# One store for both DRAM copies of a query or key half, with a channel's four copies side by side

## The chip, the cores and the metric

The kernel runs on one core of one Trainium2 chip. The metric is the device time of one execution in microseconds (us), as a median over runs. The core has five instruction queues: PE (TensorE, matmuls), DVE (VectorE), ACT (ScalarE), POOL (GpSimd) and SP (SyncE, which here issues nearly all DMAs). Each works through its instructions in the order of the program and waits on semaphores. SBUF is the on-chip memory of 128 partitions, PSUM the matmuls' accumulators, DRAM (HBM) the memory off the core.

## The reference, cut to what matters

Two layers of a hybrid block run over 1024 latent tokens and 256 context tokens. One of each layer's mixers is a differential attention of 4 heads with 2 softmaxes each, so 8 pairs of query and key with 32 channels:

```
q, k, v = split_qkv(pb, L)                 # from the shared input projection
q = apply_rope(q, rope_cos, rope_sin)      # latent tokens only
k = apply_rope(k, rope_cos, rope_sin)
keys = jnp.concatenate([k, k_c], 1)        # context keys behind the latent ones
s = jnp.einsum('bqhcd,bkhcd->bhcqk', q, k).astype(jnp.float32) * (DIFF_DK ** -0.5)
p = jax.nn.softmax(s, -1)
w = p[:, :, 0] - lam * p[:, :, 1]
return jnp.einsum('bhqk,bkhd->bqhd', w, v)
```

The other mixers are a recurrence (RG-LRU), a convolution module and a long convolution (hyena). A mixture of experts follows. All inputs are float32.

## The kernel before, in words

**Precision by halves.** A float32 number is carried as two fp32r numbers, a high half (hi) and the rest (lo). A pair's 32 channels of q are laid out as 128 rows hi, hi, lo, lo, those of k as hi, lo, hi, lo, so that one matmul over 128 rows adds all four products. That layout is made through DRAM: the tensor `qkd` has, for q (kind 0) and k (kind 1) and each of the 8 pairs, four copies of 32 channels by 1280 tokens, of 5,120 bytes a row.

**Phase 1 of a layer** (`phase1`) does the input projection, block by block of 128 columns (`win`). The matmuls (L1065) need the block's weights: a 512 KB load (`wir`, one buffer), split by ACT (`wih`, L948) and POOL (`wil`, L951), with two buffers of each half. The tokens come in groups of 512, 512 and 256 (the last is the context; in layer 1 q leaves it out). A group's result is evacuated from PSUM by a function of the block's kind. For q and k that is `qk_evac`, on 128 channels (4 pairs) at a time, so i = 0 and i = 1 for q and for k: ACT copies PSUM to `qf` (L1075), DVE shuffles and POOL and DVE apply the rotation (L1078 to L1081), ACT makes `qhi` (L948), POOL makes `qlo` (L951), and SP stores them to `qkd` (L1087), each half twice. `qhi`, `qlo` and `qf` have two buffers each, so a group's halves can be made only when the stores of the group before the last have landed.

Beside i = 0 the recurrence of the second channel block runs on DVE, POOL and ACT (`rglru`, tiles `rg_...`, L1401 to L1424), with the convolution's multiply-adds on DVE (`cacc`, L1448). Behind k of i = 1 PE goes on with the recurrence's gate (`rglru_out`, tiles `stg`, L1435 to L1437) and hyena's first block (`d_evac`, L1126), whose weights are one more `wir` load.

**Attention** (`attention`) begins with SP's loads of the constants (`lamv`, `subg`), of four `ks` (128 rows by 1280 tokens, L1269) and seven `qs` (128 by 256, L1276), all from `qkd`; a pair's 128 rows are one piece of DRAM. Then come the scores (`A`, L1186).

**What sets the order.** Every engine's program is fixed by a scheduler before the run. On SP the stores, the `wir` loads and the attention's loads stand in one order, so a load waits until all stores ahead of it have been issued.

Of the kernel before, what the change touches and what calls it, by code (L numbers as in the profile page):

```python
# [13 lines left out]
def rope_tables():  # L14
    rows = SEQ // GRID_W
    row = np.repeat(np.arange(rows, dtype=np.float32), GRID_W)
    col = np.tile(np.arange(GRID_W, dtype=np.float32), rows)
    inv = (np.float32(10000.0) ** (-np.arange(ROPE_FREQS, dtype=np.float32) / np.float32(ROPE_FREQS))).astype(np.float32)
    ang = np.concatenate([row[:, None] * inv, col[:, None] * inv], -1).astype(np.float32)   # [L, 16]
    c, s = np.cos(ang).T, np.sin(ang).T  # L20
    cos = np.tile(np.concatenate([c, c], 0), (4, 1))
    sin = np.tile(np.concatenate([-s, s], 0), (4, 1))
    return np.stack([cos, sin]).astype(np.float32)      # [2, 128, L]


def feats(L):
# [5 lines left out]
    return np.ascontiguousarray(f.T), tu                # [33, L], [L]  # L32


# Long convolution over n = 2048 points, split by k = 8 q + r, t = 256 a + p.
# Slots of 128 frequencies: 0: r0 (q < 128), 1: r4, 2-3: r1, 4-5: r2, 6-7: r3.
SLOT_R = [(0, 0), (4, 0), (1, 0), (1, 1), (2, 0), (2, 1), (3, 0), (3, 1)]
# what the butterflies give: real part and imaginary part with a sign
# [3 lines left out]
class Bank:  # L42
# [11 lines left out]
    def array(self):  # L54
        return np.ascontiguousarray(np.stack(self.blocks, 1))    # [128, nb, 128]


def long_tables():
# [3 lines left out]
    plan_f = []          # per slot: (re list, im list) of (input, half, block)  # L62
    for s, (r, qb) in enumerate(SLOT_R):
        q = np.arange(128) + 128 * qb
        th = 2 * np.pi * np.outer(p, 8 * q + r) / n       # [p, q]
        C, S = np.cos(th), np.sin(th)
        re, im = [], []
        for h in range(2):
            sl = slice(h * 128, h * 128 + 128)
            if r == 0:  # L70
                re.append(("a0", h, fw.add(C[sl])))
                m = -S[sl].copy()
                m[:, 0] = np.cos(np.pi * p[sl])           # k = 1024 in the place of Im of k = 0
# [11 lines left out]
    plan_i = {}          # per output: per half: list of (part, slot, block)  # L85
# [27 lines left out]
def short_tables():  # L113
    """n = 512, 256 times: slots 0: k < 128 (and k = 256 in Im's first row), 1: 128 <= k < 256."""
# [31 lines left out]
def pieces(tabs, long):  # L146
    """The tables' blocks in the order of their use, 8 to a piece, and where each product finds its block."""
# [24 lines left out]
def conv_tables():  # L172
    """The long convolution's tables, each frequency group's complex products as three real ones, in pieces of 4
    blocks in the order of use: forward, then inverse. Per group its pieces, each with two lists of
    (input, half, block) or (input, slot, block)."""
# [17 lines left out]
    # real inputs: both slots' real parts, then their imaginary parts  # L193
    lists = []
    for im in range(2):
        for r in (0, 4):
            C, S = trig(r, 0)
            m = -S if im else C
            if im and r == 0:
                m[:, 0] = np.cos(np.pi * p)          # k = 1024 in the place of Im of k = 0  # L200
            lists.append([(f"a{r}", h, m[half(h)]) for h in range(2)])
    fw.append(pieces_of(lists))
    # re = C (r + g i) + g (S - C) i, im = C (r + g i) - (C + S) r
# [6 lines left out]
    # inverse  # L210
# [10 lines left out]
    # R = C (Yr + Yi) - (C + S) Yi, I = C (Yr + Yi) + (S - C) Yr  # L221
# [7 lines left out]
    # the short ones  # L229
# [18 lines left out]
P = 128  # L248
# [5 lines left out]
def bcast_rows(ap1d, n, parts=P):  # L254
    """A DRAM vector of n elements as [parts, n], each partition the same."""
# [3 lines left out]
def moe_consts(K, nfix):  # L259
# [5 lines left out]
    K.j16 = c.tile([P, 8], FT, name="j16")          # j + 16  # L265
    iota(K.j16, [[1, 8]], 16)
    # falling order of the experts of the same count, those of fixed steps ahead: along the row, down the partitions
# [5 lines left out]
    # column (f, i): i in the partitions of f, -1 in the others  # L273
# [11 lines left out]
    iota(d, [[1, P]], 0, -1)                        # col - part  # L285
    K.tri = c.tile([P, P], BF, name="tri")          # tri[t', t] = t' < t
# [3 lines left out]
    K.half = c.tile([P, 1], FT, name="half")        # 1 in partitions 64 and up  # L290
# [8 lines left out]
class Router:  # L299
    """The lists of each step's tokens, from the logits of one block of tokens after the other.  # L300

    The first nfix steps take the experts of that number, the others the rest by falling count; step i has
    caps[i] rows, in blocks of 128 and, for up to 64, a last one of 64."""

    def __init__(self, K, l, NB, caps, nfix, keep, w, lists):
# [6 lines left out]
        self.OH = keep.tile([P, NB, 2, NE], BF, name="rOH")     # either choice's expert  # L312
        self.ra = keep.tile([P, NB, 2], FT, name="rra")         # its rank among the expert's
        # row + 1, token + 1, gate, the gate's low part
# [4 lines left out]
        self.cnt = keep.tile([P, 4, NE], BF, name="rcnt")       # of the rows so far, by partition  # L319
# [5 lines left out]
    def first_max(self, x, n, oh, neg):  # L325
        """One-hot oh of the first of x's largest, whose negative goes to neg"""
# [9 lines left out]
    def choose(self, b, lg):  # L336
        """The two experts of a block's tokens and their gates"""
# [9 lines left out]
        # logits of the chosen group  # L347
# [25 lines left out]
    def place(self, b):  # L373
        """A block's assignments into the lists [(value, expert), rank]"""
# [3 lines left out]
        # ranks: the rows above in the block and those of the blocks before  # L378
# [24 lines left out]
    def finish(self):  # L403
# [9 lines left out]
        # each expert's position, and the permutation  # L413
# [11 lines left out]
        # the lists as they are, and the first 64 rows of each block twice  # L425
# [11 lines left out]
        # 2**20 in rows of no assignment; half rows in blocks of 64, the first half in the lower partitions  # L437
# [6 lines left out]
        # the order of the experts last: the first rows are wanted ahead of more weights  # L444
# [11 lines left out]
    def beyond(self):  # L456
        """Whether any expert has more rows than its step"""
# [1855 lines left out]
```

## Time and profile before

| | us |
|---|---|
| median of 3 runs | 3641.28 |
| lowest and highest run | 3637.17, 3642.21 |
| span of the profiled execution, first to last instruction | 3627.2 |

Of the profiled execution the page gives the span alone; it is 14.1 us under the median of the runs, which is the work around the span together with the spread of runs. Over the span PE is busy 84%, DVE 63%, ACT 43% and POOL 20%, the DMA engines 55.8% by the hardware queue. These are means over stages with different limits. The change touches phase 1 of either layer, which in the trace lies at about 425 to 611 us and 2200 to 2367 us. A row of the trace begins with its start, then its duration; what stands in brackets behind it is the idle time of the engine before it and what ended that time. PEclk is the granted clock of TensorE as a share of its full 2.4 GHz. The DMA share is the mean busy share of the core's 16 DMA engines.

### The profile page before, as it was taken

What the parts mean: (1) busy time and instruction counts of PE and PEld (TensorE: products, weight loads), DVE (VectorE), ACT (ScalarE), POOL (GpSimd) and SP (SyncE); (2) the same over time, 40 slices, a digit from 0 to 9 for tenths busy, and PEclk for the clock granted to TensorE, in tenths of its full rate; (3) what the DMA queues carried; (4) which work ended last, traced back from release to release, by engine and by line L of the source; (5) the groups of instructions that cost most, each with busy time, mean ns of one, the idle gap of its engine ahead of it and who ended that gap; (6) DMA issues with size and microseconds to landing.
All of it is one profiled execution on the core that took longest, in us unless ns stands there. A gap on an engine that the chain in (4) does not pass through costs nothing. (4 is left out here: it accounts for less than half of the span.)

```text
span 3627.2 us, 43878 instructions
## 1 busy us (share of the span) xinstructions
PE 3060.8 (84%) x14952; PEld 2066.6 (57%) x14952; DVE 2269.4 (63%) x3297; ACT 1564.9 (43%) x2537; POOL 717.3 (20%) x579
## 2 busy tenths in 40 slices
PE   5898775998789699999998587789888799899993
PEld 1246664676568354577554465557667665465552
DVE  6675873887768444375543678478886753356626
ACT  4234342774324233365543454267433344345523
POOL 2213441001320101111110444300230111111102
PEclk9999987999999699999999798889989899999996
DMA  6751224223566789996978512221446389978796
GB/s 189 225 196 49 69 85 159 81 73 128 168 197 218 241 299 325 355 327 235 319 259 329 176 38 93 83 83 65 151 152 216 130 300 372 384 276 292 267 348 246
DMA packets 415023, 743.33 MB, mean 205 GB/s; under 512 B 45867, under 2 KB 180888, under 8 KB 414794
## 3 DMA queue, kind: packets, MB, share of 16 engines
q1 hardware_dynamic: 397194, 702.69, 55.8%
q0 software_dynamic: 17600, 37.79, 3.1%
q8 instruction: 119, 1.95, 0.2%
q14 instruction: 110, 0.90, 0.1%
HBM read 656.13 MB, written 105.30 MB: 210 GB/s over the span
## 5 line engine op out<-in xcount | busy, mean ns | idle before, releaser
L679 DVE TENSOR_TENSOR wl<-wr,wh 128x1024 fp32r<-128x1024 f32 (+1 forms) x440 | 516.2, 1202 | 392.0 <-ACT wh L678 379.4
L678 ACT ACTIVATE wh<-wr 128x1024 fp32r<-128x1024 f32 (+1 forms) x440 | 442.2, 1038 | 328.7 <-PE mm L730 190.7
L1065 PE MATMUL mm<-hh,wih 128*128 128x512 f32 (+1 forms) x752 | 292.6, 390 | 51.5 <-ACT stg L1126 39.6
L734 PE MATMUL mm<-wr,xl 128*64 128x512 f32 x1216 | 328.0, 609 | 4.2 <-DVE xl L690 1.6
L1065 PE MATMUL mm<-hh,wil 128*128 128x512 f32 (+1 forms) x752 | 290.6, 387 | 18.0 <-POOL wil L951 17.4
L730 PE MATMUL mm<-wh,xh 128*128 128x512 f32 x704 | 289.5, 412 | 6.7 <-ACT wh L678 6.2
L1065 PE MATMUL mm<-hl,wih 128*128 128x512 f32 (+1 forms) x752 | 290.9, 387 | 1.5 <-DVE hl L951 0.9
L730 PE MATMUL mm<-wl,xh 128*128 128x512 f32 x704 | 278.3, 395 | 3.6 <-DVE wl L679 3.5
L730 PE MATMUL mm<-wh,xl 128*128 128x512 f32 x704 | 277.1, 394 | 0.0
L790 POOL DMA_INDIRECT fd<-ot,ridx x82 | 94.5, 1152 | 839.7 <-ACT ot L786 262.0
L1448 DVE SCALAR_TENSOR_TENSOR cacc<-cu,cw,cacc 128x1295 f32<-128x1295 f32 (+1 forms) x120 | 194.3, 1619 | 1.9
L1065 PEld LDWEIGHTS mm<-hh,wih 128*128 128x128 f32 x752 | 147.5, 196 | 83.1 <-ACT stg L1126 43.2
L671 POOL DMA_INDIRECT gb<-h2d,ridx x82 | 98.8, 1205 | 462.6 <-PE tr L698 192.7
L730 PEld LDWEIGHTS mm<-wh,xh 128*128 128x128 f32 x704 | 133.4, 190 | 92.6 <-issue 45.1
L1196 DVE TENSOR_REDUCE m<-A 128x1 f32<-128x1024 f32 x128 | 156.1, 1220 | 44.0 <-PE A L1186 36.8
L951 POOL TENSOR_TENSOR wil<-wir,wih 128x1024 fp32r<-128x1024 f32 x34 | 91.4, 2688 | 465.4 <-ACT wih L948 409.4
L734 PEld LDWEIGHTS mm<-wr,xl 128*64 128x64 f32 x1216 | 96.0, 137 | 141.7 <-issue 126.7
L1065 PEld LDWEIGHTS mm<-hh,wil 128*128 128x128 f32 x752 | 147.4, 196 | 48.5 <-POOL wil L951 20.0
L1065 PEld LDWEIGHTS mm<-hl,wih 128*128 128x128 f32 x752 | 148.2, 197 | 31.3 <-issue 6.0
L780 PE MATMUL mm<-wr,hl 128*64 128x512 f32 x608 | 153.9, 602 | 0.0
L730 PEld LDWEIGHTS mm<-wl,xh 128*128 128x128 f32 x704 | 133.8, 190 | 30.6 <-DVE wl L679 6.6
L1241 ACT ACTIVATE wT<-TR 128x512 f32<-128x512 f32 (+1 forms) x200 | 104.9, 524 | 107.0 <-PE TR L1236 97.7
(491 smaller groups left out, 6493.0 us busy)
## 6 DMA issues: line engine op xcount, KB each, us to landing
wr<-in_moe_w_gate_dram SPq DMA_DIRECT2D x256, 512.0 KB
wr<-in_moe_w_up_dram SPq DMA_DIRECT2D x256, 512.0 KB
wr<-in_moe_w_down_dram SPq DMA_DIRECT2D x256, 512.0 KB
wada<-in_w_ada_dram SPq DMA_DIRECT2D x48, 512.0 KB
tabc<-in_k_t_c_dram SPq DMA_DIRECT2D x88, 256.0 KB
wir<-in_w_in_dram SPq DMA_DIRECT2D x40, 512.0 KB
wr<-in_w_ada_dram SPq DMA_DIRECT2D x32, 512.0 KB
ks<-qkd SPq DMA_DIRECT2D x16, 640.0 KB
```

Source lines behind the costliest of these rows:

```text
L671: self.K.nc.gpsimd.indirect_dma_start(out=g[s, :D // (1 + h)], out_offset=None, in_=self.h2d[h], in_offset=bass.IndirectOffsetOnAxis(ap=id ...
L678: nc.scalar.activation(hi, src, AF.Copy)
L679: nc.vector.tensor_tensor(lo, src, hi.bitcast(FT), op=OP.subtract)
L730: nc.tensor.matmul(ps[b][w], x(k), y[:, kk], start=(k == 0 and c == 0), stop=(k == 7 and c == 2))
L734: nc.tensor.matmul(ps[b][0][w * 64:(w + 1) * 64], self.XT[n0 + b](k), raw[w][:, kk], start=(k == 0), stop=(k == 7))
L780: nc.tensor.matmul(po[b][0][o * 64:(o + 1) * 64], HT[b][:, k], raw[:, o], start=(k == 0), stop=(k == 3))
L790: s = nc.gpsimd.indirect_dma_start(out=self.fd[h], out_offset=bass.IndirectOffsetOnAxis(ap=ridx[r], axis=0), in_=ot[r], in_offset=None, bo ...
L951: (eng or nc.vector).tensor_tensor(lo, src, hi.bitcast(FT), op=OP.subtract)
L1065: nc.tensor.matmul(p[:, :n], a[:, k], b[:, k, t0:t0 + n], start=(k == 0 and a is wh and b is hh), stop=(k == 7 and a is wl))
L1196: nc.vector.tensor_reduce(m[:, c, 1:2], A[c], axis=AX.X, op=OP.max, negate=True)
L1241: nc.scalar.activation(o, i_, AF.Copy)
L1448: nc.vector.scalar_tensor_tensor(a, u[:, j:j + N], cw(j), a, op0=OP.mult, op1=OP.add)
```

## The change

The DRAM tensor's copy dimension goes behind the channel, so the four copies of a channel lie beside each other. One store then writes both copies of a half, from a view of the tile that repeats each partition's row twice: copies 0 and 1 (hi) or 2 and 3 (lo) for q, copies 0 and 2 or 1 and 3 for k. The loads name the dimensions in the new order; a pair's 128 rows are one piece of DRAM as before, in an order by channel and then copy, the same for q and k.

```diff
-        self.qkd = self.dram.tile([2, 8, 4, 32, T0], FT, name="qkd")
+        self.qkd = self.dram.tile([2, 8, 32, 4, T0], FT, name="qkd")
...
             self.split(q[:, :n], hi[:, :n], lo[:, :n], eng=nc.gpsimd)
-            for s, t in enumerate((hi, hi, lo, lo) if kind == 0 else (hi, lo, hi, lo)):
-                nc.sync.dma_start(self.qkd[kind, i * 4:(i + 1) * 4, s, :, t0:t0 + n], t[:, :n].bitcast(FT))
+            o = self.qkd[kind, i * 4:(i + 1) * 4].rearrange("h r s t -> (h r) s t")
+            for s, t in enumerate((hi, lo)):
+                c = slice(2 * s, 2 * s + 2) if kind == 0 else slice(s, None, 2)
+                nc.sync.dma_start(o[:, c, t0:t0 + n], t[:, None, :n].bitcast(FT).to_broadcast([P, 2, n]))
...
-                    nc.sync.dma_start(k.bitcast(FT), self.qkd[1, pr * 4 + hc].rearrange("s r t -> (s r) t"))
+                    nc.sync.dma_start(k.bitcast(FT), self.qkd[1, pr * 4 + hc].rearrange("r s t -> (r s) t"))
...
                         nc.sync.dma_start(q.bitcast(FT), self.qkd[0, pr * 4 + hc, :, :, t0:t0 + 256]
-                                          .rearrange("s r t -> (s r) t"))
+                                          .rearrange("r s t -> (r s) t"))
```

Only SP's program differs: 2262 rows where there were 2286. The order of PE, DVE, ACT and POOL is the same row by row, but for line numbers (three higher behind the change). On SP, layer 0, i = 0, behind the loads of v's weights (`wir` of 128x4x256), the stores of q and the next blocks' weight loads stood so (sizes are those of the side in DRAM; x2 means twice in a row):

```order
L1097 DMA wir<-in_w_in_dram 128x4x256 x2
L1087 DMA qkd<-qhi 4x32x512 x2
L1087 DMA qkd<-qlo 4x32x512 x2
L1052 DMA wir<-in_w_in_dram 128x8x128
L1087 DMA qkd<-qhi 4x32x512 x2
L1087 DMA qkd<-qlo 4x32x512 x2
L1087 DMA qkd<-qhi 4x32x256 x2
L1087 DMA qkd<-qlo 4x32x256 x2
L1052 DMA wir<-in_w_in_dram 128x8x128
```

and now, at the same place, stand:

```order
L1100 DMA wir<-in_w_in_dram 128x4x256 x2
L1090 DMA qkd<-qhi 128x2x512
L1090 DMA qkd<-qlo 128x2x512
L1052 DMA wir<-in_w_in_dram 128x8x128
L1090 DMA qkd<-qhi 128x2x512
L1090 DMA qkd<-qlo 128x2x512
L1090 DMA qkd<-qhi 128x2x256
L1090 DMA qkd<-qlo 128x2x256
L1052 DMA wir<-in_w_in_dram 128x8x128
```

Nothing has moved past anything else; two stores of 4 by 32 rows have become one of 128 by 2 rows. On SP, layer 0, i = 1, the last two groups of k, hyena's weight load and a load of a bias stood so:

```order
L1087 DMA qkd<-qhi 4x32x512
L1087 DMA qkd<-qlo 4x32x512
L1087 DMA qkd<-qhi 4x32x512
L1087 DMA qkd<-qlo 4x32x512
L1087 DMA qkd<-qhi 4x32x256
L1087 DMA qkd<-qlo 4x32x256
L1087 DMA qkd<-qhi 4x32x256
L1087 DMA qkd<-qlo 4x32x256
L1052 DMA wir<-in_w_in_dram 128x8x128
```

and now:

```order
L1090 DMA qkd<-qhi 256x1x512
L1090 DMA qkd<-qlo 256x1x512
L1090 DMA qkd<-qhi 256x1x256
L1090 DMA qkd<-qlo 256x1x256
L1052 DMA wir<-in_w_in_dram 128x8x128
```

Here k's stores are written as 256 rows, since its two copies and the channels have one common step in DRAM. The weight load still stands behind all of k's stores.

## Rows read from the trace of the kernel before

**Rows 1.** Who waited for `qkd`, whole span: us in total, times.

```profile
  POOL qlo L951: 42.0, 8
  ACT qhi L948: 34.1, 5
```

**Rows 2.** Busy time by stretch: us, PE, PEld, DVE, ACT, POOL, PEclk, DMA share, GB/s.

```profile
525.00:550.00 25.00, 25.00 (x134) 21.64 (x134) 13.92 (x15) 5.29 (x9) 16.40 (x10) 1.00 0.31 103
...
575.00:600.00 25.00, 5.62 (x16) 4.13 (x15) 4.23 (x3) 3.82 (x6) 3.36 (x2) 0.59 0.31 110
...
2325.00:2350.00 25.00, 7.26 (x21) 5.40 (x21) 1.52 (x2) 4.69 (x7) 2.02 (x2) 0.64 0.32 112
```

**Rows 3.** DMA, 2312 to 2328, in 40 slices: the stores of `qkd`.

```profile
GB/s 102 102 102 102 102 102 102 102 102 102 102 102 102 102 102 102 102 102 102 102 102 102 102 102 102 102 102 102 102 102 102 102 102 102 102 102 102 102 97 102
...
q1 hardware_dynamic: 823, 1.64, 26.3%
```

**Rows 4.** DMA, 2427 to 2430: one store `pd<-stg` of 128x512, 256 KB.

```profile
GB/s 0 0 0 0 0 0 0 0 0 0 0 0 0 137 273 328 410 355 410 410 410 382 301 82 0 0 0 0 0 0 0 0 0 0 0 0 0 0 0 0
```

**Rows 5.** DMA, 533 to 541: the first stores behind a pause (issued from 533.56).

```profile
GB/s 5 0 0 0 0 0 0 0 31 41 41 10 0 31 0 10 10 61 61 72 51 72 102 92 102 102 92 102 102 102 102 102 102 102 102 102 102 102 102 102
```

**Rows 6.** SP's queue in order of time: three weight loads and one store.

```profile
427.51 0.37 SPq L1097 DMA_DIRECT2D wir<-in_w_in_dram  x1
...
572.16 2.43 SPq L1087 DMA_DIRECT2D qkd<-qlo  x1
...
584.00 1.82 SPq L1052 DMA_DIRECT2D wir<-in_w_in_dram  x1
...
2338.95 1.79 SPq L1052 DMA_DIRECT2D wir<-in_w_in_dram  x1
```

**Rows 7.** ACT in order of time.

```profile
431.03 1.06 ACT L948 ACTIVATE wvh<-wir 128x1024 fp32r<-128x1024 f32 x1 [2.33 <-DMA wir<-in_w_in_dram]
...
543.62 0.60 ACT L1075 ACTIVATE qf<-mm 128x512 f32<-128x512 f32 x1 [0.68 <-POOL qlo L951]
552.70 0.63 ACT L948 ACTIVATE qhi<-qf 128x512 fp32r<-128x512 f32 x1 [8.48 <-DMA qkd<-qhi]
...
592.61 1.06 ACT L948 ACTIVATE wih<-wir 128x1024 fp32r<-128x1024 f32 x1 [17.00 <-DMA wir<-in_w_in_dram]
...
2303.22 0.58 ACT L1075 ACTIVATE qf<-mm 128x512 f32<-128x512 f32 x1
...
2307.76 0.58 ACT L1075 ACTIVATE qf<-mm 128x512 f32<-128x512 f32 x1
...
2347.59 1.06 ACT L948 ACTIVATE wih<-wir 128x1024 fp32r<-128x1024 f32 x1 [17.47 <-DMA wir<-in_w_in_dram]
```

**Rows 8.** POOL: the split of a weight load.

```profile
2348.73 2.36 POOL L951 TENSOR_TENSOR wil<-wir,wih 128x1024 fp32r<-128x1024 f32 x1 [17.27 <-ACT wih L948]
```

**Rows 9.** PE in order of time: hyena's block and the first scores.

```profile
566.18 0.80 PE L1065 MATMUL mm<-hh,wih 128*128 128x512 f32 x1 [6.69 <-ACT wih L948]
...
594.87 0.80 PE L1065 MATMUL mm<-hh,wih 128*128 128x512 f32 x1 [19.38 <-ACT stg L1126]
...
610.75 1.19 PE L1186 MATMUL A<-ks,qs 128*128 128x512 f32 x2 [3.62 <-DMA qs<-qkd]
...
2323.76 0.80 PE L1065 MATMUL mm<-hh,wil 128*128 128x512 f32 x1 [6.16 <-POOL wil L951]
...
2349.68 0.80 PE L1065 MATMUL mm<-hh,wih 128*128 128x512 f32 x1 [17.74 <-ACT stg L1126]
...
2366.86 1.19 PE L1186 MATMUL A<-ks,qs 128*128 128x512 f32 x2 [9.53 <-DMA qs<-qkd]
```

**Rows 10.** DVE in order of time: waits beside i = 0.

```profile
455.18 0.01 DVE L1078 LOAD_MASK_SELECT qsw<-qf  x1 [3.31 <-ACT qf L1075]
...
475.14 1.74 DVE L1401 SCALAR_TENSOR_TENSOR rg_u<-xa,pp,rg_u 128x512 f32<-128x512 f32 x1 [6.22 <-POOL rg_u L1399]
...
2243.92 1.28 DVE L1421 TENSOR_TENSOR_SCAN h<-rg_r,h,rg_t 128x512 f32<-128x512 f32 x1 [4.68 <-POOL rg_t L1417]
```

## The prediction

> **What bounds the kernel now.** The change touches only the stores and loads of `qkd`, so the first view to read is who waits for that tensor. POOL waits 42.0 us and ACT 34.1 us for the stores to free `qlo` and `qhi` [rows 1]. Those waits count only where PE's work hangs on them, so the second view is busy time by stretch. PE is full from 525 to 550, and then has 5.62 us of work in the 25 us up to 600; in layer 1 it has 7.26 us in the 25 us up to 2350 [rows 2]. No compute engine is full there: DVE, ACT and POOL are each under 5 us of 25. The only thing that runs without a break is DMA, at a share of 0.31 and 0.32.
>
> The third view is DMA in such a stretch. The stores move a steady 102 GB/s at a share of 26.3% [rows 3], close to 4 of 16 engines. A store of 256 KB at that rate takes 2.57 us, and one issue keeps SP for 2.43 us [rows 6]: SP is held back by the stores. A store with as many bytes and the same 2 KB pieces, but with 128 rows as its outer dimension, runs at up to 410 GB/s and is through in about 0.8 us (11 slices of 0.075 us) [rows 4]. So neither DRAM nor the size of a piece sets the 102 GB/s. The old store's outer dimension in DRAM is 4 heads, and 4 engines are busy.
>
> The chain at the end of phase 1 is then: the last stores are late, so SP issues hyena's weight load only at 584.00 (layer 1: 2338.95) [rows 6]; ACT stands 17.00 (17.47) us for it and splits at 592.61 (2347.59) [rows 7]; PE's block waits 19.38 (17.74) us, and the loads for attention come behind it on SP, so the first scores start at 610.75 (2366.86) [rows 9].
>
> **The change, part by part.** *Stores.* 88 stores become 44 of twice the bytes: no byte less. Both halves of each i have about 5 MB to write (layer 0: 2 x 1280 tokens x 128 channels x 4 copies x 4 bytes = 5.24 MB, 51 us at 102 GB/s). Their new outer dimension is 128 rows, or 256 for k. The nearest row is the 128-row store at 410 GB/s, and I take that: a 512 KB store in 1.3 to 1.6 us. No row shows a source that repeats each row twice, nor 256 rows against 128 partitions, so the ends for the stores' rate stay open: 410 GB/s above, and below a split by the two copies, half of 102, which is 51 GB/s. The Trainium skill (DMA: Bandwidth & Descriptors, section Why a DMA increments its semaphore by 16 and not by 1) says that the engine count is the largest number up to 16 that divides the outermost dimension above one on both sides; by it the old stores get 4 and both new forms 16, so the sum would be as here and the low end would not occur.
>
> *Second half of phase 1 (i = 1), layer 0.* I replay the end with the engines' own times. Layer 1 shows an undisturbed group of k: from one `qf` to the next 4.54 us (2303.22 to 2307.76) [rows 7]. Layer 0's first k group starts at 543.62; in the trace its `qhi` comes at 552.70 after 8.48 us on the store [rows 7]. At 4.54 us a group the third `qf` is at 552.7. Behind it stand ACT's split of 1.06 [rows 7], POOL's of 2.36 [rows 8] and the last `qlo` of half a group, with hand-overs 5 us: the last half is ready at 557.7. SP then issues two stores and the weight load, 1 us at the 0.37 of an unhindered issue [rows 6]: 558.7. An unhindered weight load reaches its user in 3.5 us (issue 427.51, use 431.03) [rows 6, 7], where the trace has 8.6 now. So the split moves from 592.61 to 562.2: **30.4 us** earlier. What follows is unchanged: gate, constants, `ks`, `qs`, scores, in the same 18 us from the split (592.61 to 610.75). PE can follow: 6.69 + 19.38 + 3.62 = 29.7 us of that are its own waits [rows 9], and the rest it gets from the clock, which in 575 to 600 is granted at 0.59 [rows 2].
>
> *Second half, layer 1.* The groups' `qf` start at 2303.22, so the third is at 2312.3; 5 us, 1 us and 3.5 us behind it is 2321.8, against 2347.59: **25.8 us**. PE's waits there are 6.16 + 17.74 + 9.53 = 33.4 us [rows 9].
>
> *First half (i = 0).* Here the recurrence and the convolution keep DVE busy, so only DVE's own waits can turn into time. Two in layer 0 go back to a weight load queued among stores: 3.31 us, where ACT brings `qf` late because it stands for the load, and 6.22 us, where POOL's split is late for the same reason. In layer 1 it is 4.68 us [rows 10]. I take all three, **14.2 us**; the ends are 0 and this. It carries over, because PE is full from 525 to 550 [rows 2] and whatever starts it earlier ends it earlier.
>
> *Loads.* A pair's 128 rows are one piece of DRAM as before: nothing. *Fewer issues:* SP saves 44 issues of 0.4 us, hidden, as SP waits for data in both halves.
>
> *What is late next:* at the end of i = 1 the evacuation itself, at 4.54 us a group, and then the attention's loads. No other engine's order changes, so the stages behind start earlier by the same amount and last as long.
>
> *Sum:* 30.4 + 25.8 + 14.2 = 70.4 us. The span of the profile would go from 3627.2 to 3556.8; the runs' median of 3641.28 lies 14.1 above that span, and less 70.4 it is **3571 us**.
>
> As a bound on the gain: all of PE's waits in either second half are 29.7 + 33.4 = 63.1 us [rows 9]. Its 12.9 us of work in the two slow stretches ran at 0.59 and 0.64 of the clock [rows 2], worth an estimated 5 at the full one. With the first halves that is 82 us, 3559; I allow 11 us more for gaps and slow work outside these rows, so 3548.
>
> **The rivals.**
>
> *B, a slow start for each store.* The first stores behind a pause were issued from 533.56, and their rate stays at 10 to 60 GB/s until about 537 [rows 5]: some 3.5 us in which little is moved. If the new stores each pay this one after the other, a group's two stores take 8 us with their own bytes, more than the 4.54 of the evacuation. Three groups then lose 3.5 us each, 10 in either second half, and the first halves give nothing: 70.4 - 21 - 14.2 = 35 us, so 3606. Against it: in a burst the rate is flat at 102 [rows 3], so the start is paid once, and the 128-row store shows none [rows 4]. The Trainium skill (same page, section Anatomy of one DMA) has for the software path about 2.0 us fixed and bytes over 436 GB/s: an estimate of 3.2 us per new store and 6.4 per group, in series, and by it three groups lose 5.6 us in either second half, which makes 3582. The same formula gives the old store 2.6 us, so on it alone the old pace would not be a matter of engines; the share of 26.3% speaks against it.
>
> *C, no gain.* The stores still run on 4 engines, or the weight load has another cause for its 17 us. For: bytes and issue order are the same. Against: the 8.48 us wait of `qhi` names the store, and 4 as an outer size is gone. It gives 3641, within 7.
>
> *D, slower.* The DMA splits by the two copies, and 2 engines move 51 GB/s. Each half's 5.24 MB (layer 1: 4.72) then takes 103 us (92) where it takes 51 (46). The second halves lose 51 and 46, so 3738 at the least; the first halves may add as much where they find no pause. It decides as soon as the stores' rate is under about 100 GB/s. For: the repeated row is a form no row shows. Against: the outermost dimension is the rows, and the old stores' split went by the outermost.
>
> *E, more than the bound*, under 3548, if the shifted stages also take fewer waits of their own, for instance a fuller clock in attention.
>
> **How the numbers follow.** The forecast, anywhere from 3548 to 3595 (the upper end is the two second halves at 8.6 us for a weight load, 10 us less, and nothing from the first halves): 0.70. B and gains between, 3595 to 3634: 0.17. C: 0.04. D: 0.05. E: 0.04. The range 3548 to 3610 holds the forecast and most of B, so about 0.84, and leaves out C, D, E and the tail of B. A measurement of this kernel tells 0.2%, 7.3 us, from no change. Faster: 0.70 + 0.17 + 0.04 = 0.91; same 0.04; slower 0.05.
>
> **What would show it.** Stores at a DMA share near 1 and over 300 GB/s in short bursts, with long empty stretches between; POOL's and ACT's waits for `qkd` together under 10 us instead of 76; the third `qf` of k about 9 us behind the first; the weight load's wait at the end under 5 us; first scores some 40 us earlier in layer 0 and 70 in layer 1, and the same 70 at the end. It is wrong if the stores' share stays at 0.26 (C) or falls to half (D), if `qhi` still waits for its stores with the engines idle (B), or if the scores start early and the end does not.

## The result, and the profile after

The changed kernel takes **3578.34 us** (median of 4 runs, 3570.96 to 3583.19), the kernel before, run beside it, 3639.23 us (median of 4, 3636.11 to 3642.21). The ratio is 0.9836, with a 95% interval from 0.9813 to 0.986: some 61 us less. The forecast was 3571, the range 3548 to 3610.

A run's time lies 1.9 us above its span here (3583.19 and 3581.3 in the profiled one), so most of the 14.1 us that stood between the span of before and its median was spread from run to run, and not work around the span. The two single spans differ by less than the runs do (3627.2 to 3581.3 is 45.9 us), and the comparison below goes by stretches. Who waited for `qkd` in the profile after:

```profile
L1090 SPq DMA_DIRECT2D qkd<-qhi x22: 359/513/598, 440.5 to 2286.2; - x22
...
  PEld A L1189: 13.6, 2
  PE A L1189: 13.0, 2
```

The 76 us that POOL and ACT waited for the stores [rows 1] are gone. What is left are the first scores of either layer, which wait for loads. An issue of a store with twice the bytes keeps SP for 0.51 us in the median. Before it was 1.90 us for the same tile, and 2.43 for the store in [rows 6]:

```profile
L1087 SPq DMA_DIRECT2D qkd<-qhi x44: 503/1904/3669, 437.3 to 2335.0; - x44
```

Now DMA from 545 to 557, the end of i = 1 in layer 0, where k's stores of 256 rows stand, in 40 slices of 0.3 us (busy tenths, GB/s, share of 16 engines):

```profile
DMA  9999699999999800000199999999999620008981
GB/s 326 331 329 336 232 362 404 389 382 348 403 362 403 314 27 0 0 0 0 68 403 362 403 362 376 375 362 396 372 335 341 205 65 0 0 0 300 328 236 24
...
q1 hardware_dynamic: 2508, 3.06, 71.0%
```

Before, a stretch like this was one flat line at 102 GB/s and a share of 26.3% [rows 3]. Now the engines are full at 330 to 400 GB/s, and then have nothing to do until the evacuation brings the next halves. The stores of 128 rows, those of q, run at the same rate; the first two of i = 1, from 530 to 540 in slices of 0.25 us:

```profile
GB/s 0 0 0 0 0 213 393 385 385 385 328 8 0 0 0 0 0 0 0 0 66 377 393 393 393 385 90 0 0 0 0 0 0 0 0 0 0 0 0 41
```

The empty slices show that the stores no longer set the pace. ACT, which makes the halves and splits the weights, in order of time (start, us; in brackets the idle time before it and what ended it):

```profile
540.48 0.60 ACT L1075 ACTIVATE qf<-mm 128x512 f32<-128x512 f32 x1 [0.68 <-POOL qlo L951]
...
545.09 0.58 ACT L1075 ACTIVATE qf<-mm 128x512 f32<-128x512 f32 x1
...
549.63 0.37 ACT L1075 ACTIVATE qf<-mm 128x256 f32<-128x256 f32 x1
...
560.09 1.06 ACT L948 ACTIVATE wih<-wir 128x1024 fp32r<-128x1024 f32 x1 [6.44 <-DMA wir<-in_w_in_dram]
...
2294.39 1.06 ACT L948 ACTIVATE wih<-wir 128x1024 fp32r<-128x1024 f32 x1 [6.78 <-DMA wir<-in_w_in_dram]
```

Groups of k follow each other in 4.61 and 4.54 us; the wait of 8.48 us on the store [rows 7] has no successor. The split for hyena's block waits 6.44 and 6.78 us for its load instead of 17.00 and 17.47. The load's issue on SP, in order of time:

```profile
555.24 0.97 SPq L1052 DMA_DIRECT2D wir<-in_w_in_dram  x1
...
2289.63 0.60 SPq L1052 DMA_DIRECT2D wir<-in_w_in_dram  x1
```

From issue to use it is 4.85 us in layer 0 and 4.76 in layer 1 (8.61 and 8.64 before, [rows 6, 7]). PE in order of time, hyena's block and the first scores, against [rows 9]:

```profile
562.05 0.50 PE L1065 MATMUL mm<-hh,wih 128*128 128x512 f32 x1 [1.59 <-ACT stg L1129]
...
571.74 0.58 PE L1065 MATMUL mm<-hh,wih 128*128 128x256 f32 x1 [3.96 <-ACT stg L1129]
...
578.05 1.02 PE L1189 MATMUL A<-ks,qs 128*128 128x512 f32 x2 [1.95 <-DMA qs<-qkd]
...
2296.47 0.50 PE L1065 MATMUL mm<-hh,wih 128*128 128x512 f32 x1 [1.73 <-ACT stg L1129]
...
2313.33 1.22 PE L1189 MATMUL A<-ks,qs 128*128 128x512 f32 x2 [11.08 <-DMA qs<-qkd]
```

In layer 0 PE's block waits 1.59 us where it waited 19.38, in layer 1 1.73 where it waited 17.74. Busy time by stretch after (columns as in [rows 2]):

```profile
525.00:550.00 25.00, 25.00 (x133) 21.56 (x132) 13.89 (x16) 5.72 (x12) 18.18 (x12) 1.00 0.63 216
550.00:575.00 25.00, 19.45 (x98) 16.49 (x97) 5.10 (x7) 7.50 (x12) 6.99 (x4) 0.93 0.57 203
575.00:600.00 25.00, 17.69 (x105) 9.28 (x105) 16.96 (x24) 13.25 (x31) 2.37 (x1) 0.80 0.68 219
```

The hole of 575 to 600, with 5.62 us of PE work at a granted clock of 0.59, is filled: 17.69 us at 0.80.

For all kernels of this study the program can be cut at five events of the trace: SP's first store of i = 0 and of i = 1, and PE's first scores, in either layer. Lengths in us, one profiled execution each, worked out from the starts of those instructions (for the change the range of three executions):

| kernel | L0: i=0 to i=1 | L0: i=1 to scores | scores L0 to store L1 | L1: i=0 to i=1 | L1: i=1 to scores | scores to end |
|---|---|---|---|---|---|---|
| before | 96.3 | 77.2 | 1598.7 | 84.5 | 72.9 | 1260.3 |
| change | 89.9 to 90.2 | 47.0 to 48.0 | 1601.9 to 1604.6 | 84.1 to 85.7 | 46.8 to 47.6 | 1263.5 to 1268.0 |
| e1 wide, unmerged | 89.9 | 48.5 | 1599.7 | 84.1 | 48.3 | 1259.4 |
| e2 narrow | 96.2 | 77.1 | 1601.4 | 85.4 | 72.8 | 1258.0 |
| e3 two heads | 142.6 | 125.5 | 1603.1 | 111.5 | 113.3 | 1266.1 |
| e4 loads first | 89.9 | 38.3 | 1615.5 | 85.0 | 38.9 | 1272.5 |
| e5 first half only | 90.4 | 76.8 | 1595.3 | 84.1 | 72.6 | 1261.9 |
| e6 second half only | 96.2 | 47.9 | 1590.3 | 84.5 | 47.4 | 1259.2 |
| e7, e11 constants later | 90.0, 90.4 | 43.2, 43.8 | 1595.0, 1597.6 | 84.1, 84.2 | 44.4, 43.8 | 1270.4, 1266.5 |
| e9 split on VectorE | 83.6 | 51.5 | 1584.0 | 88.7 | 50.8 | 1265.2 |
| e10 both | 84.3 | 46.9 | 1584.7 | 88.7 | 47.7 | 1267.7 |

In the profile of the result the four stretches of phase 1 changed by -6.3, -29.6, +1.2 and -25.3 us: -60.0 together, and the runs' medians differ by 61. The two long stretches were not touched. Single executions of kernels in which PE, DVE, ACT and POOL run in the same order (before, change, e1, e2, e5, e6) spread from 1590.3 to 1604.6 us and from 1258.0 to 1268.0 there. The change lies at the upper end in all its three executions; whether it costs some us there stays open.

### The profile page after: what moved, and what is told of

It is laid out like the page before. It is cut to its first block, busy times and chain, and to the rows that moved or that the text cites. A ratio compares the mean times of both kernels' runs of the same rounds, so it can differ in the third digit from the quotient of the medians.

```text
span 3581.3 us, 43827 instructions
## 1 busy us (share of the span) xinstructions
PE 3073.7 (86%) x14952; PEld 2071.0 (58%) x14952; DVE 2274.8 (64%) x3297; ACT 1564.7 (44%) x2537; POOL 722.5 (20%) x579
```

## The experiments

Three theories were to be told apart for the gain in the second halves. **Engines:** the outermost dimension of the store's side in DRAM (4 heads, now 128 or 256 rows) sets how many DMA engines work. **Merging:** half as many stores, so half the fixed costs. **Layout:** a channel's copies beside each other. For the first halves the question was why 14.2 us of waits gave so little.

**e1: the new layout and 128 rows, but one store per copy.**

```diff
-            for s, t in enumerate((hi, lo)):
-                c = slice(2 * s, 2 * s + 2) if kind == 0 else slice(s, None, 2)
-                nc.sync.dma_start(o[:, c, t0:t0 + n], t[:, None, :n].bitcast(FT).to_broadcast([P, 2, n]))
+            for s, t in enumerate((hi, hi, lo, lo) if kind == 0 else (hi, lo, hi, lo)):
+                nc.sync.dma_start(o[:, s, t0:t0 + n], t[:, :n].bitcast(FT))
```

> The new layout, but every copy is a store of its own again: 88 stores, each of 128 rows. Theory A (a store runs on as many engines as its outermost dimension allows, and the old outer dimension of 4 heads is the whole cause): as the change, 3565 to 3590, stores in bursts over 300 GB/s, no wait of POOL or ACT for the stores. Rival B (the number of stores counts: SP's issues and the DMAs in flight): as before, 3632 to 3646. Rival C (the copies' place in DRAM counts): as the change too; the next run tells A from C.

3580.27 us (4 runs, 3569.24 to 3586.7), ratio 0.9848 [0.9821, 0.9876]: not to be told from the change. Who waited for `qkd` in its trace, the stores' part:

```profile
L1089 SPq DMA_DIRECT2D qkd<-qhi x44: 319/398/1622, 444.2 to 2290.1; - x44
...
  POOL qlo L951: 1.5, 1
```

88 stores of 256 KB do as well as 44 of 512 KB, and each keeps SP for 0.40 us in the median. Merging is worth nothing that can be measured.

**e2: the new layout, one store per copy, and 4 heads outermost.** A channel block gets a 33rd row, which nobody uses, so that the heads can't be folded into the rows.

```diff
-        self.qkd = self.dram.tile([2, 8, 32, 4, T0], FT, name="qkd")
+        self.qkd = self.dram.tile([2, 8, 33, 4, T0], FT, name="qkd")
...
+            for s, t in enumerate((hi, hi, lo, lo) if kind == 0 else (hi, lo, hi, lo)):
+                nc.sync.dma_start(self.qkd[kind, i * 4:(i + 1) * 4, 0:32, s, t0:t0 + n], t[:, :n].bitcast(FT))
```

> The new layout with one unused channel row behind each pair's 32, so that four heads and 32 rows can't be taken as 128 rows; every copy a store of its own with 4 heads outermost: 88 stores as before, in the new place. A: as before, 3632 to 3646, stores at 102 GB/s and a DMA share of 0.26. C (place in DRAM): as the change, 3570 to 3590. B (number of stores): as before.

3634.76 us (median of 9 runs), ratio 1.0001 [0.9988, 1.0015]: the time of before. So are its waits for `qkd`:

```profile
  POOL qlo L951: 42.0, 8
  ACT qhi L948: 34.2, 5
```

and the share of DMA from 560 to 575, in the midst of its stores:

```profile
q1 hardware_dynamic: 1006, 1.48, 26.6%
```

To a tenth the waits are [rows 1], and the share is near the 26.3% of [rows 3]. Between e1 and e2 layout (but for the unused row), bytes and number of stores are the same; what differs is the outermost dimension, 128 rows or 4 heads, and with it go all 55 us. The layout alone gives nothing.

**e3: each store of e2 cut into two of 2 heads.**

```diff
+                for g in range(0, 4, 2):
+                    nc.sync.dma_start(self.qkd[kind, i * 4 + g:i * 4 + g + 2, 0:32, s, t0:t0 + n],
+                                      t[g * 32:g * 32 + 64, :n].bitcast(FT))
```

> As the run with 4 heads outermost, but each store split into two of 2 heads: the same bytes in 176 stores. A: 2 engines, 51 GB/s; the two second halves lose 51 and 46 us against before, the first halves up to as much where no pause covers it: 3735 to 3830. B (a price per store, the same for each): 88 stores more cost what 44 fewer gave twice over, some 120 us: 3760, but then the rate in a burst would not be a steady 51 GB/s and the DMA share not 0.13. If both are wrong and bytes alone count: 3639.

3804.55 us (2 runs), ratio 1.0465 [1.0444, 1.0486]: some 169 us slower than before. The scheduler also shifted rows of the other engines in this kernel, so its evidence is the rate and the share, not the time. DMA from 650 to 666 in its trace:

```profile
GB/s 51 51 51 51 51 51 51 51 51 51 51 51 51 51 51 51 51 51 51 51 51 51 51 51 51 51 51 51 51 51 51 51 51 51 51 51 51 51 46 51
...
q1 hardware_dynamic: 413, 0.82, 13.1%
```

Half the outermost dimension, half the rate and half the share: 51 GB/s at 13.1% for 2, 102 GB/s at 26.3% for 4 [rows 3]. If the shares mean 2 and 4 engines of 16 (13.1% is 2.1, 26.3% is 4.2), that is 25.5 GB/s for each in both; 16 times that is 408, and the wide store of [rows 4] peaks at 410. A price per store, the same for each, falls: its expectation had ruled out a steady 51 GB/s. The Trainium skill (DMA: Bandwidth & Descriptors, section Why a DMA increments its semaphore by 16 and not by 1) takes the largest number up to 16 that divides the outermost dimensions above one as the number of engines; the traces agree at 2, at 4, and, with busy tenths of 9, at 256 rows; the stores of 128 rows moved up to 393 GB/s. The run also shows what the slow rival of the prediction costs if it does occur: the waits of POOL and ACT for `qkd` are 174.1 and 120.4 us.

**e5 and e6: the change in one half alone.** Two tensors in DRAM, one for each i; one is stored in the new way, the other, with 33 rows, in e2's way.

```diff
-        self.qkd = self.dram.tile([2, 8, 32, 4, T0], FT, name="qkd")
+        self.qkd = [self.dram.tile([2, 4, r, 4, T0], FT, name=f"qkd{i}") for i, r in enumerate((32, 33))]
...
+            if i == 0:
```

> The change for i = 0 alone; the stores of i = 1 keep 4 heads outermost, one copy each (their pairs lie in a DRAM tensor of their own with an unused row behind each pair). By the prediction's sum the first halves give 14.2 us: 3620 to 3625. By the stage lengths of the changed kernel's trace (first store of i = 0 to first store of i = 1: 6.4 us shorter in layer 0, 1.2 us longer in layer 1) it is 5 us: 3628 to 3634. Scores as late behind the first store of i = 1 as before: 77 and 73 us.

3628.7 us (7 runs), ratio 0.9983 [0.9965, 1.0001], so about 6 us, with an interval from 0 to 13. The stretches agree: 90.4 instead of 96.3 in layer 0, 84.1 instead of 84.5 in layer 1.

> The change for i = 1 alone, the stores of i = 0 as before. By the prediction's sum 56.2 us less than before, by the stage lengths of the changed kernel's trace 54.9: both 3578 to 3585. If the two halves lean on each other (the engines still busy with old stores when the new ones come), the gain is under 45 us: 3590 and more. Scores 47 to 49 us behind the first store of i = 1 in either layer.

3575.73 us (4 runs), ratio 0.9854 [0.9832, 0.9876], about 53 us. Both second halves are as short as in the change (47.9 and 47.4), the first halves as long as before (96.2 and 84.5). By the ratios the two parts are 53 + 6 = 59 of 61; by the medians against the runs of before beside them they are 60 + 7 = 67. Within this spread they add up to the whole.

**Why the first halves gave 6 us and not 14.2.** The forecast's three waits of DVE did go. Busy time by stretch, layer 1's and layer 0's first half (first store of i = 0 to that of i = 1), columns as in [rows 2]; before:

```profile
2209.40:2293.90 84.50, 68.88 (x381) 57.00 (x382) 73.76 (x72) 38.42 (x52) 38.58 (x25) 0.87 0.24 82
437.30:533.60 96.30, 73.36 (x414) 61.09 (x414) 78.73 (x71) 39.72 (x55) 46.31 (x27) 0.87 0.27 89
```

and in the third execution of the change (e12):

```profile
437.90:528.10 90.20, 74.31 (x409) 61.95 (x409) 81.50 (x71) 40.08 (x55) 48.85 (x27) 0.88 0.28 95
```

In layer 0 DVE's idle time falls from 17.57 to 8.70 us, by 8.9 of the 9.53 us that were forecast. But the same 71 instructions are busy 2.77 us longer, most of it in `cacc` (43.7 us before, 46.2 in e12). In layer 1 of the result's profile it is 2.99 us (76.75 us instead of 73.76), while the idle time falls by only 1.8, from 10.74 to 8.95. Which ones get longer there, tells the view by groups (busy us, mean ns, then idle time); before, layer 1's first half:

```profile
L1401 DVE SCALAR_TENSOR_TENSOR rg_u<-xa,pp,rg_u 128x512 f32<-128x512 f32 x12 | 9.8, 820 | 2.0 <-POOL rg_u L1399 2.0
```

after:

```profile
L1404 DVE SCALAR_TENSOR_TENSOR rg_u<-xa,pp,rg_u 128x512 f32<-128x512 f32 x12 | 17.1, 1423 | 2.0 <-POOL rg_u L1402 2.0
```

The same twelve instructions take 820 ns before and 1423 after (another group, `cacc`, gets 4.1 us back). In e5, with the change in the first half alone, they take 1252, in e6, with the second half alone, 821: it is the change in the first half that does it. POOL and DVE in order of time show how. Before, layer 1:

```profile
2238.50 0.74 DVE L1401 SCALAR_TENSOR_TENSOR rg_u<-xa,pp,rg_u 128x512 f32<-128x512 f32 x1
...
2238.61 2.84 POOL L951 TENSOR_TENSOR wil<-wir,wih 128x1024 fp32r<-128x1024 f32 x1 [2.36 <-ACT wih L948]
```

after:

```profile
2193.21 2.72 POOL L951 TENSOR_TENSOR wil<-wir,wih 128x1024 fp32r<-128x1024 f32 x1
...
2193.72 2.76 DVE L1404 SCALAR_TENSOR_TENSOR rg_u<-xa,pp,rg_u 128x512 f32<-128x512 f32 x1
...
2206.90 3.36 POOL L951 TENSOR_TENSOR wil<-wir,wih 128x1024 fp32r<-128x1024 f32 x1
...
2207.93 2.88 DVE L1404 SCALAR_TENSOR_TENSOR rg_u<-xa,pp,rg_u 128x512 f32<-128x512 f32 x1
...
2215.27 0.72 DVE L1404 SCALAR_TENSOR_TENSOR rg_u<-xa,pp,rg_u 128x512 f32<-128x512 f32 x1
```

An `rg_u` alone takes 0.72 us. Beside POOL's split it takes 2.76 and 2.88, and ends a little behind it: 2196.48 behind 2195.93, 2210.81 behind 2210.26, both by 0.55. Before, the split ran from 2238.61 to 2241.45, and 2.21 us of it lay in the 4.68 us in which DVE stood idle up to 2243.92 [rows 10]; the `rg_u` that had begun ahead of it took its 0.74 us. In layer 0 it is `cacc` that meets the splits. Before, a split lay in the wait of 6.22 us up to 475.14 [rows 10]:

```profile
449.66 1.55 DVE L1448 SCALAR_TENSOR_TENSOR cacc<-cu,cw,cacc 128x1295 f32<-128x1295 f32 x1
...
472.01 2.35 POOL L951 TENSOR_TENSOR wil<-wir,wih 128x1024 fp32r<-128x1024 f32 x1 [5.72 <-ACT wih L948]
```

and in e12:

```profile
450.14 2.80 POOL L951 TENSOR_TENSOR wil<-wir,wih 128x1024 fp32r<-128x1024 f32 x1
...
450.65 3.65 DVE L1451 SCALAR_TENSOR_TENSOR cacc<-cu,cw,cacc 128x1295 f32<-128x1295 f32 x1
...
464.80 2.84 POOL L951 TENSOR_TENSOR wil<-wir,wih 128x1024 fp32r<-128x1024 f32 x1
...
465.96 3.05 DVE L1451 SCALAR_TENSOR_TENSOR cacc<-cu,cw,cacc 128x1295 f32<-128x1295 f32 x1
```

A `cacc` alone takes 1.55 us; these two are 2.10 and 1.50 longer and overlap the split by 2.29 and 1.68. The two `rg_u` are 2.04 and 2.16 longer and overlap it by 2.21 and 2.33. Each time the loss is the overlap less 0.17 to 0.19 us, nearly but not "exactly" the overlap, as the expectation below has it. So the time of POOL's split was part of a wait of DVE before, and is a longer instruction of DVE now. The Trainium skill (SBUF — State Buffer, section Who interferes with whom) states that a VectorE instruction with two inputs in SBUF contends with a GpSimd instruction that reads SBUF, and that the order of issue decides which of them blocks; these rows agree, with 2.76 us for an `rg_u` that began 0.51 us behind a split, and 2.84 us for a split that began 0.11 us behind an `rg_u`, where [rows 8] has 2.36.

**e9: the change, and those four splits a layer on VectorE.** If the split costs DVE its 2.4 us in either form, DVE should do better to do it itself.

```diff
-                            self.win(l, w, [4 + i], hs, allg, [self.qk_evac(wq, 0, i, rope)])
-                            self.win(l, w, [6 + i], hs, GROUPS, [self.qk_evac(wq, 1, i, rope)])
+                            self.win(l, w, [4 + i], hs, allg, [self.qk_evac(wq, 0, i, rope)], None, nc.vector)
+                            self.win(l, w, [6 + i], hs, GROUPS, [self.qk_evac(wq, 1, i, rope)], None, nc.vector)
```

> The changed kernel, and the low halves of the weights of q's and k's blocks (the tiles wil of these four blocks a layer) are subtracted on VectorE instead of GpSimd; the scheduler shifts some rows of the other engines with it. The first half of phase 1 (first store of i = 0 to first store of i = 1) lasts 90 us in layer 0 and 84 to 86 us in layer 1 with the change, 96 and 84.5 before. Theory L: in the traces a VectorE instruction is longer by exactly the time that it overlaps an instruction of GpSimd (rg_u 0.72 us alone, 2.76 us beside 2.21 us of wil), so removing a VectorE wait only moves GpSimd's 2.4 us split from the wait into VectorE's own time. Then with the splits on VectorE, at about 1.1 us each (cacc of the same 128x1024 size, alone), either first half with two or three splits in it falls by 2 to 4 us, the rg_u group's mean falls from 1.25 to 1.42 us to under 0.95 us, and the whole time falls by 4 to 8 us against the change beside it (some 3569 to 3573). Theory W: the first half is set by chains of waits and not by VectorE's time; both lengths stay within 1 us and the time within 3 us, or it rises by the 1.1 us a split that VectorE now does itself.

> The changed kernel itself, as the measure for the three beside it: 3577 us, 0.983 of the kernel before. In its first half of layer 1 VectorE's group rg_u should again take 1.25 to 1.42 us each.

3566.88 us (5 runs, 3559.07 to 3571.86; ratio 0.9808 [0.9792, 0.9825]) against 3572.88 for the change beside it (5 runs, 3567.28 to 3576.53; 0.982 [0.9806, 0.9833]): 6.0 us less in the medians, as theory L had it, though the intervals overlap. Layer 0, first store to scores:

```profile
439.90:523.50 83.60, 69.63 (x410) 59.26 (x410) 75.00 (x67) 37.07 (x51) 43.24 (x25) 0.93 0.24 82
523.50:575.00 51.50, 42.52 (x208) 35.80 (x207) 21.24 (x22) 12.35 (x20) 23.91 (x13) 0.93 0.64 227
```

and the second half in e12, whose first half is above:

```profile
528.10:576.10 48.00, 43.64 (x215) 37.08 (x213) 14.35 (x18) 12.45 (x20) 21.08 (x13) 0.93 0.61 216
```

Both halves together take 135.1 us, in three executions of the change 136.9 to 138.2, so 2 to 3 us are gained. They can only be taken together, as two `cacc` and other DVE work moved from the first half into the second. DVE's busy time did not fall: 96.2 us in both halves, where e12 has 95.9. The two splits in it took 3.5 us (2.31 and 1.21, not 1.1 each), and the rest of DVE's work some 3 us less (0.7 of it a shuffle that moved out); so the 2 to 3 us came out of DVE's waits. The other part of the expectation missed: the mean of `rg_u` stays above 0.95 us (1023 and 1059 ns), since the rest of POOL's work still meets DVE, and so does the split: one `wil` on DVE took 2.31 us beside a `qlo` of POOL. In layer 1 the program's order shifted as well, and single stretches can't be compared; from the scores of layer 0 to those of layer 1 it took 1723.5 us, the change 1735.0 to 1735.6. But e6, with the change's order of PE, DVE, ACT and POOL, took 1722.1, so these 11.5 us can't be put down to the edit. The rows above show the mechanism of theory L for the splits; its price, that DVE saves time by taking them over, isn't shown.

**e4, e7 and e11: what is late next.** With the stores out of the way the first scores wait for `qs`, 11.08 us in layer 1. SP issues 5 loads of constants ahead of the attention's 4 loads of k and first 4 of q. e4 interleaves k's and q's loads and puts the constants behind them; e7 puts only the constants behind (the first and the last line of this edit).

```diff
-        nl, subg = self.lam_vec(l, w)
...
-                for hc in range(4):
-                    k = w.tile([P, T0], FR, name="ks", bufs=4)
...
+                        if t0 == 0:
+                            k = w.tile([P, T0], FR, name="ks", bufs=4)
...
+        nl, subg = self.lam_vec(l, w)
```

> The change, with attention's first loads in the order of their use (k and q of a pair in turn) and the loads of the constants behind them. Theory: what is late after the change is the way from the last weight load to the first scores, in which SP issues five constants, four loads of k and then those of q. PE's gap ahead of the first scores (11.08 us in layer 1, 1.95 in layer 0) shrinks by 5 to 8 and by 1 to 2 us, so 6 to 10 us less than the change: about 3570. Rival: the scores are held by the landing of the first k alone, and the order behind it does nothing: as the change, within 4.

3576.59 us (4 runs), ratio 0.9834 [0.9817, 0.9852]. The second halves shrink by 9 us each (38.3, 38.9), yet the time is the change's. A part of the 9 us is the mark and no gain: the scheduler had reordered PE's rows with the loads, and the first scores now stand ahead of most of hyena's block:

```profile
572.74 1.19 PE L1188 MATMUL A<-ks,qs 128*128 128x512 f32 x2 [6.31 <-DMA qs<-qkd]
...
573.95 0.63 PE L1065 MATMUL mm<-hh,wil 128*128 128x512 f32 x1
...
2312.17 1.19 PE L1188 MATMUL A<-ks,qs 128*128 128x512 f32 x2 [5.51 <-DMA qs<-qkd]
...
2313.37 0.63 PE L1065 MATMUL mm<-hh,wil 128*128 128x512 f32 x1
```

PE's gap shrank by 5.6 us in layer 1, as forecast, and grew by 4.4 in layer 0, where it was to shrink. A mark behind both is DVE's first output of the attention (`yt`): from the first store of i = 1 it comes at 70.4 and 74.8 us, in the change at 75.6 to 76.6 and 77.1 to 78.2. So some 5 to 6 and 2 to 3 us were won there. Where they were lost again isn't shown; the two long stretches (1615.5 and 1272.5 us) are longer than any of the change's, with another order of rows and in the slowest of the four runs.

> The change, with the five loads of attention's constants moved behind the first loads of k and q, whose order stays; the rest of the program keeps its order but for a few small rows. Theory: SP's time for the five constants (2.4 us) and their small pieces in DMA delay the first scores in both layers, and since the order of attention is left alone this time the gain isn't given back: the stretch from the first store of i = 1 to the first scores falls from 47.6 to 42 to 45 us, and the time by 4 to 10 us against the change run beside it. Rival: attention's first units are paced by something else and the time is that of the change, within 3 us.

> The change once more, for its spread and as the partner of the run before: 3570 to 3585. If the 3 to 4 us that layer 0's start, the rest of layer 0 and the tail each lost in the first trace are chance, they come out otherwise here; if they follow from the change, they stand again (first store at 440, 1602 us from the scores of layer 0 to the first store of layer 1, 1268 us from the scores of layer 1 to the end).

e7 takes 3569.94 us (5 runs; 0.9824 [0.9811, 0.9838]), the change beside it 3576.77 (5 runs; 0.9833 [0.9815, 0.9852]). Of what the change's first trace had lost, the start was chance (first store at 438.2 and 437.9 in e8 and e12, 437.3 before), the 1602 us stood again (1604.6, 1602.8), and the tail came out between (1264.4, 1263.5).

> The kernel with attention's constants issued behind the first loads, once more: 3570 us if the 6.8 us against the change beside it were no chance, within 3 us of the change beside it if they were. The stretches from the first store of i = 1 to the scores should be 43 to 45 us again, where the change has 47 to 48.

3566.41 us (5 runs; 0.9811 [0.9797, 0.9825]), against 3572.88 of e12. Twice the median is lower, by 6.8 and 6.5 us, and twice the stretch to the scores is 2 to 5 us shorter in either layer; single runs of both overlap. In layer 1 the order of PE is the change's, and PE waits 8.03 and 7.54 us for `qs` instead of 10.65 to 11.08. In layer 0 part of it is the mark again: the first scores stand ahead of most of the matmuls of hyena's last group. By the first `yt` e7 and e11 win 4 to 5 us in layer 0 (71.2, 71.5) and 0 to 3 in layer 1 (76.9, 75.1).

**e10: both edits.**

> The changed kernel with both: attention's constants issued behind the first loads of keys and queries, and the low halves of q's and k's weights on VectorE. If the two gains add, it stands under the change by 6 (constants) plus 4 to 8, at 3562 to 3568 us. If the attention's order shifts, as in the run with the loads ahead, it gives the gain back and stays at about 3577 us.

**3552.31 us** (5 runs, 3548.9 to 3555.84), ratio to before 0.9765 [0.9751, 0.9778]. This interval lies clear of the change's (0.9806 to 0.9833): 20.6 us below it, and the fastest kernel of this study. It is 8 us more than the two edits gave singly (6.0 and 6.5). In layer 0 the two edits add up: from the first store of i = 0 to the first `yt` it takes 159.3 us, the change 165.5 to 166.8, e9 163.6, e7 and e11 161.2 and 161.9. Which stretch holds the 8 us can't be told: its profiled execution also started 3.9 us earlier (first store at 434.0 instead of 437.9), and it was as much ahead at its first `wil` (273.6 instead of 277.5), before anything that either edit touches.

One more idea, a second buffer of `wir` so that hyena's weights are loaded before the last stores, wasn't tried; what it is worth stays open.

## Why the prediction was right, and where its sizes were off

**The bound.** Right: the stores ran on as many engines as the old outer size of 4 allowed, and e1, e2 and e3 show that this size, and neither the merging nor the layout, makes the time. The chosen end for the rate, the 128-row store at 410 GB/s, was the right one: up to 393 GB/s with 128 rows, 330 to 400 with 256.

**The second halves.** 30.4 and 25.8 us were forecast; 29.6 and 25.3 were measured, in e6 some 53 us by the ratio of the runs and 60 by their medians. The replay at 4.54 us a group held (4.61, 4.54). The one term that was off is the weight load at 3.5 us, which took 4.85 and 4.76; it had been taken from a load that had DMA to itself (0.52 MB moved from 427.5 to 431, which is the load), while here 1.25 MB move from 555.2 to 560.1, the last store and the gate's stores among them. The load's wait at the end therefore stayed at 6.44 and 6.78, where the prediction wanted it under 5. The 18 us from split to scores held: 560.09 to 578.05 is 17.96. The first scores came 32.7 us earlier in layer 0 and 53.5 in layer 1, where 40 and 70 were named as signs; the first halves, and the spread of the start and of the long stretch between, are the difference.

**The first halves.** This is the mis-sized step. "I take all three, 14.2 us" rested on DVE's waits turning into time in full. The waits went (8.9 us in layer 0, and the 4.68 in layer 1), but DVE's own instructions became 2.8 and 3.0 us longer, chiefly where they now meet POOL's splits, and in layer 1 two other waits of DVE grew: for POOL's `rg_u` from 0.93 to 2.18 us, for ACT's `rg_i` from 0.1 to 1.8 (1.0 in e12, 0.1 in e8). What came out is a gain of 6.1 to 6.4 us in layer 0 and of -1.2 to 0.4 us in layer 1, where the lower end that the prediction named, 0, was the nearer one.

**The sum.** 70.4 forecast, 61 measured. Of the 9.4 us between, some 8 are the first halves (14.2 less 6) and 1.3 the second ones (56.2 less 54.9); with 51 to 68 us as the runs' interval this split is a rough one.

**The rivals.** B, a slow start for each store, did not occur: in the slices above, the rate goes from 0 over 68 to 403 GB/s within two slices of 0.3 us, and the first store of i = 1, issued at 530.46, moves 213 and then 393 GB/s from 531.25 on, where the first stores at this place stayed at 10 to 60 for some 3.5 us before [rows 5]. (B's own terms also give more than its 8 us: two stores at 3.5 us of start and 1.3 of bytes are 9.6 us a group, which makes some 3615 and not 3606.) The estimate of 3.2 us for each new store, one after the other, falls with it: in the first fourteen slices, 4.2 us at 352 GB/s in the mean, 1.48 MB were moved, a group's two stores of 512 KB and what stood ahead of them, where the estimate has 6.4 us for the two alone. C fell by the waits, D by the share of 9 tenths. E did not occur in the change; e10 comes within 5 us of its bound, but with other edits.

## What to carry to other kernels

A DMA share that stands still at 1/4 or 1/8 while every compute engine idles meant here that few engines carried the transfers. In such a case look at the outermost dimension of the DRAM side first, before merging or moving anything: 2 and 4 ran at 51 and 102 GB/s here, 128 and 256 at 330 to 400. A load that a critical block needs, queued behind such stores on one in-order queue, pays for them twice: the rate and the queue. A stretch between two events is only comparable while no work has moved across its ends: in e4 the first scores came 9 us sooner, and some 3 of that in layer 0 and 6 in layer 1 were work put behind them. Waits of a busy VectorE are not yet time to be won: look what GpSimd does in them, because work that ran in the gap may block VectorE's next instruction when it comes earlier.

## What was not expected of the hardware

- The rate of a narrow store is a plain multiple: 51 GB/s with 2 outer rows, 102 with 4, so 25.5 GB/s for each, whatever the pieces' place in DRAM (e2 has the old share, 26.6%, in the new layout).
- The slow first 3.5 us of the narrow stores behind a pause [rows 5] were not seen with 128 rows at the same place. Why they are there with 4 stays open.
- A 0.72 us instruction of VectorE took 2.76 and 2.88 us beside GpSimd's split, a 1.55 us one 3.65 and 3.05. All four lost their overlap with the split, less 0.17 to 0.19 us.
